# Linear attention's queries and keys as a 1024-column unit by row form, turned on PE

## The chip, the cores and the metric

The kernel runs on one core of a Trainium2 chip. The metric is the device time of one execution in microseconds (us): the median of three runs, 2145.22 us for the kernel before (2144.92 to 2146.12).

The engines are named as the profile names them: PE multiplies matrices (PEld is its weight load), DVE and ACT work elementwise, POOL is used for small work and for issuing DMAs that add, SP issues the loads. PE writes to PSUM, which has eight banks of 128 partitions x 512 words.

## The reference

Two layers over a residual stream x of 256 rows and 2048 columns, all in float32:

```python
def hybrid_layer(x, ...):
    h = rms_norm(x, attn_norm)
    proj = h @ w_in                       # 2048 x 6160
    g_q, g_k, g_v, g_gate, g_lr, s_q, s_k, s_v = split(proj)
    #  512, 512, 1024, 1024,  16, 1024, 1024, 1024 columns
    log_a = log_sigmoid(g_lr @ w_gate_up + b_gate) / 16
    o_gla = gla_chunked(g_q, g_k, g_v, log_a)       # 8 heads, chunks of 64 rows
    o_gla = rms_norm(o_gla, gla_out_norm) * silu(g_gate)
    sq, sk = rms_norm(s_q, sb_q_norm), rms_norm(s_k, sb_k_norm)
    o_sb = rms_norm(stick_breaking_attention(sq, sk, s_v), sb_out_norm)
    x = x + concat(o_gla, o_sb) @ w_o
    hm = rms_norm(x, mlp_norm)
    return x + square(relu(hm @ w_up)) @ w_down     # 2048 -> 8192 -> 2048
```

Linear attention needs its queries and keys with the head's 64 columns on the partitions, multiplied by exponentials of the running sum of log_a: q by exp(b), k by exp(-b), and k by exp(b_last - b).

## The kernel before, in words

**Products.** Every float32 factor is split in a high part (ACT copies it, rounded, into `whi`) and a low part (DVE subtracts, into `wlo`). A product of a 128 x 128 block of h with a 128 x 512 block of weights is three matmuls: high x high, high x low, low x high.

**Plain units** (`unit`, lines 577 to 579) make 256 rows x up to 512 columns of a projection: 16 blocks of h's columns, two halves of rows, three matmuls, so 96 matmuls. A unit loads four blocks of 1 MB and has eight chunks of 12 matmuls. After each chunk `tick()` runs what `after(n, fn)` has put n chunks later: attention's own steps lie between the chunks in this way. The order of PE, DVE and ACT here is that of the tile scheduler.

**The column form** (`unit_t`, lines 624 and 628) makes 256 columns of linear attention's queries or keys already turned: weights are the stationary factor, the high and low parts of h stand side by side as one 512-column moving factor, and the low weights meet the high part in a 256-column matmul. That is 32 pairs of a 512- and a 256-column matmul. `join` adds the two halves (a copy on ACT, an addition on DVE).

**The ordered lists.** The gate, the output projection and the MLP of a layer, and in layer 0 two units for layer 1 ("iv": stick-breaking values, "ik": its keys), run as units of 1024 columns whose order on PE, DVE and ACT is planned (`Plan`: each piece has a length, dependencies and a due time; PE's and SP's pieces keep their order, DVE's and ACT's go by due time) and written out by hand (`manual_schedule`). `STEPS` is the order of the steps of the eight pairs of blocks of such a unit. For a pair in `FAST` (1, 3, 5, 6) seven products stand for eight: DVE makes sums of weight blocks (line 1097), and the operand keeps sums of its own blocks (`forms`, lines 436 to 454). For a pair in `ADDED` (2, 7) the low part is made without DVE: ACT writes the negated high part (line 1274, `dlo`), and a DMA issued by POOL adds the weights to it (line 1277). So a unit has 64 products less 4: 180 matmuls. Three buffers `raw` and two `raw2` hold loaded weights, five `whi` and four `wlo` the parts. Each unit ends in a tail: DVE combines the eight banks, and for "iv" and "ik" ACT multiplies by the row's inverse norm.

**Layer 0's mixer** begins the program: x comes in four parts of 512 columns, each is turned on PE (line 469) and split, between the first chunks. Its units in order: stick-breaking values (512), keys (512), gate rank with the first queries (272), queries (256), values, keys, queries (512 each), four column-form units, linear attention's values (two of 512), and half of the output gate. Layer 1's mixer is the same without values and keys, which "iv" and "ik" have left. The gates' exponentials are multiplied by the row's inverse norm on POOL, for which `row_of` turns that norm into a row on PE (line 535).

Squares for the heads' norms are made in `head_sums` (line 645) on DVE; normalised queries and keys (line 651) are turned on PE (line 688).

Of the kernel before, what the change touches and what calls it, by code (L numbers as in the profile page):

```python
# [17 lines left out]
P = 128  # L18
# [5 lines left out]
FAST = (1, 3, 5, 6)  # L24
ADDED = (2, 7)
BIG = ("up", "down", "iv", "ik")
# [16 lines left out]
C_SQ, C_SK, C_SV = 3088, 4112, 5136  # L43

# [100 lines left out]
def trunk_kernel(  # L145
# [60 lines left out]
    ATT = ("wg", "ident16", "mask16", "tri", "nones", "gmask", "reset", "v4", "lr", "lrT", "ha", "hh", "hl", "hA", "on", "dec", "S", "kdz", "row", "bc")  # L206
# [15 lines left out]
    def mlp_psum():  # L222

        open_scope("psum", m=1)
        unused.update((m, new_bank(m)) for m in (1, 6, 5, 7, 2, 4, 3, 8))
# [5 lines left out]
    open_scope("sbuf", att=1)  # L231
# [99 lines left out]
    def load_small():  # L331
        load_gains(1, (
            ("sq", sb_q_norm, 1), ("sk", sb_k_norm, 1), ("mlp", mlp_norm, KT),
            ("gla", gla_out_norm, 1), ("so", sb_out_norm, 1),
        ))
        load_gate_up(0)
# [85 lines left out]
    def forms(op, i, t, tag):  # L422
# [18 lines left out]
        def high():  # L441
# [6 lines left out]
            todo.append((op.pair(i), t))  # L448
# [9 lines left out]
    def operand_parts(op, n, h2, key, l, place):  # L458
# [30 lines left out]
        def scaled():  # L489
            t = tmp("t2", [P, 2, T], bufs=T2)  # L490
# [6 lines left out]
    def norm_operand(op, n, key, l, sums=False):  # L497
        for h2 in range(2):
            turn, high, low, scaled = operand_parts(op, n, h2, key, l, ps_tile)
            turn()  # L500
            if sums and fast(2 * n + h2):
                for part in forms(op, 2 * n + h2, scaled(), "sxh"):
                    part()
            else:
                high()
                low()
# [288 lines left out]
    hT = Operand()  # L795
    ssq = new_ssq()
    st = {}
    his = []
    load_x(0, parts=2)
    load_gains(0, (("attn", attn_norm, KT),))  # L800
    wait_on_x(WARM0)
    first = [operand_parts(hT, 0, h2, "attn", 0, ps_tile) for h2 in range(2)]
    for turn, _, _, _ in first:
        turn()
    st["first"] = turn_gains(0)
    for _, high, low, _ in first:
        high()
        low()
    wait_on_x(WARM1)

    for l in range(DEPTH):
        wl = w_in[l]
        mixed = Operand()
        nxt = {}

        if l == 0:
            hooks = {}

            def next_x(n):
                load_x(n)  # L820
                with tc.issue_after(st["mm"]):
                    norm_operand(hT, n, "attn", 0)

            for n, at in ((1, (0, 0)), (2, (0, 1)), (3, (1, 1))):
                hooks[at] = lambda n=n: next_x(n)

            def begin():
                st["rst"] = norm_finish(ssq)

            for n in range(4):  # L830
                after(6 + n, lambda n=n: norm_squares(n, ssq))
            after(10, begin)
            after(2, build_constants)
            after(7, load_small)
            after(11, finish_small)
            uv = unit(
                hT, wl, 0, C_SV, 512, hooks=hooks, fine=1,
                order=lambda i, k: his[4 * i + (3 if i else max(1, k))],
            )
            v = tmp("v4", [P, NT, 512], bufs=2)  # L840
            after(3, lambda a=uv, b=v: values(a, b))
        else:
            open_scope("sbuf", att=1)
            att_psum()
            load_gate_up(l)
            after(2, build_constants)
            v = natural["iv"][0]

        def sb_heads(g, qT, kT, v, first):

            state = {}

            def scores(hp):
                state[hp] = sb_scores(qT, kT, 2 * hp)
                after(3, lambda: weights(hp))

            def weights(hp):
                state[hp] = sb_weights(*state[hp])
                after(1, lambda: outs(hp))

            def outs(hp):
                po = ps_tile()
                for j in range(2):
                    sb_out(po, j, state[hp], v, 2 * hp + j)
                o = norm_pair(po)
                after(3, lambda: to_operand(mixed, 4 + 2 * g + hp, o, gain("so", l)))

            for hp in range(2):
                after(first[hp], lambda hp=hp: scores(hp))


        if l == 0:
            uk = unit(hT, wl, 0, C_SK, 512)
            rst = st["rst"]
            kT = act_tile(F32)
            sb_qk(uk, 0, 4, 0, rst, None, kT, 4)
        else:
            rst = st["rst"]
            kT = act_tile(F32)
            after(2, lambda kT=kT: sb_qk(None, 0, 4, 0, rst, None, kT, 5, natural["ik"][0]))  # L880
# [22 lines left out]
        def gates(b):  # L903
# [24 lines left out]
            def fl(t):  # L928
                return t[:, bs, :].rearrange("p e t -> p (e t)")
# [788 lines left out]
```

## Time and profile before

| what | value |
|---|---|
| runs | 2144.92, 2145.22, 2146.12 us |
| profiled execution | 2145.51 us, span 2143.8 us |
| mixer of layer 0 (without its first unit) | 33.9 to 295.9 us of the span |
| list of layer 0, up to the first steps of layer 1's values | 295.9 to 1080.4 us |
| mixer of layer 1 | 1162.6 to 1360.2 us |
| list of layer 1 | 1360.2 to 2139.7 us |
| clock granted to TensorE | 1.00 throughout |
| mean DMA rate | 224 GB/s |

A row of a timeline has the start in us from the span's beginning, the length in us, engine, line, operation, written tile <- read tiles, shapes and count; in brackets the idle time before it and what ended it. A matmul's length overlaps the next one's: what it costs PE is the distance to the next start. A row of stage times has the stretch, its length, and the busy time and count of each engine, then granted clock, share of the DMA engines and GB/s. In a row of waits stand the total, the number and the longest.

### The profile page before, as it was taken

The numbers are of one execution on the slowest core, as the hardware profiler recorded it, in microseconds if no ns is written. First come the engines' busy times: TensorE is split into PE (matmuls) and PEld (weight loads), VectorE is DVE, ScalarE is ACT, GpSimd is POOL, SyncE is SP. The second block draws the span as 40 slices with busy tenths as digits, with TensorE's granted clock in tenths as the row PEclk, the third lists the DMA queues.
The fourth block names the chain that finished last, engine by engine and source line by source line (L and its number), as shares of the span: only waits on it lengthen the run. The fifth ranks groups of instructions, "written<-read, shape, count | busy, mean of one in ns | idle before, by whom it ended". The sixth has DMA issues, their size and how long they took to land.

```text
span 2143.8 us, 28392 instructions
## 1 busy us (share of the span) xinstructions
PE 2134.1 (100%) x10239; PEld 1780.4 (83%) x10239; DVE 1892.3 (88%) x2533; ACT 1471.4 (69%) x1889; POOL 157.0 (7%) x210
## 2 busy tenths in 40 slices
PE   9999999999999999999999999999999999999999
PEld 7988888888888888888878888888888888888887
DVE  5677669999999999999998875799999999999998
ACT  5555456678677677678776654667876776776775
POOL 0020000000000000000001200000000000000000
PEclk9999999999999999999999999999999999999999
DMA  6655456688888888888886544657888888888886
GB/s 229 196 158 167 158 197 196 196 245 265 244 253 246 260 251 243 273 236 255 238 242 170 176 159 158 202 173 228 253 243 274 236 261 247 248 247 253 255 249 182
DMA packets 169105, 480.37 MB, mean 224 GB/s; under 512 B 9370, under 2 KB 34530, under 8 KB 168964
## 3 DMA queue, kind: packets, MB, share of 16 engines
q1 hardware_dynamic: 149380, 407.24, 56.4%
q0 software_dynamic: 19584, 71.31, 17.6%
q8 instruction: 80, 1.31, 0.2%
q14 instruction: 61, 0.50, 0.1%
HBM read 405.12 MB, written 2.10 MB: 190 GB/s over the span
## 4 chain that ended last, share of the span: by engine, by line
PE 94%; DVE 3%; issue 1%; ACT 1%; DMA 0%; POOL 0%; DVEq 0%; ACTq 0%
PE acc L577 4%; PE acc L579 4%; PE acc L578 4%; PE acc L624 3%; PE acc L628 1%; DVE wlo L1268 1%; DVE wlo L560 0%; DVE xb L1097 0%; PE ps L1065 0%; DMA raw<-in_w_in_dram 0%; PE ps L1058 0%; PE ps L742 0%; PE ps L1015 0%; PE ps L688 0%; PE ps L706 0%
## 5 line engine op out<-in xcount | busy, mean ns | idle before, releaser
L1264 ACT ACTIVATE whi<-raw 128x1024 fp32r<-128x1024 f32 (+1 forms) x768 | 738.9, 976 | 314.4 <-issue 45.3
L1268 DVE TENSOR_TENSOR wlo<-raw,whi 128x1024 fp32r<-128x1024 f32 (+1 forms) x632 | 689.1, 1097 | 65.6 <-ACT whi L1264 54.0
L560 DVE TENSOR_TENSOR wlo<-raw,whi 128x1024 fp32r<-128x1024 f32 (+2 forms) x162 | 182.2, 1131 | 93.3 <-ACT whi L558 93.2
L558 ACT ACTIVATE whi<-raw 128x1024 fp32r<-128x1024 f32 (+2 forms) x162 | 156.0, 968 | 153.4 <-PE acc L579 109.3
L1277 POOL DMA_DIRECT2D dlo<-raw x136 | 117.2, 862 | 1587.6 <-ACT dlo L1274 837.7
L1264 ACT ACTIVATE whi<-ts 128x1024 fp32r<-128x1024 f32 x144 | 152.7, 1061 | 73.6 <-DVE ts L1097 4.0
L577 PE MATMUL acc<-whi,act 128*128 128x512 f32 (+2 forms) x512 | 191.4, 374 | 0.0
L578 PE MATMUL acc<-wlo,act 128*128 128x512 f32 (+2 forms) x512 | 186.5, 364 | 0.1
L579 PE MATMUL acc<-whi,act 128*128 128x512 f32 (+2 forms) x512 | 186.5, 364 | 0.0
L1268 DVE TENSOR_TENSOR wlo<-ts,whi 128x1024 fp32r<-128x1024 f32 x144 | 175.5, 1219 | 10.2 <-ACT whi L1264 8.5
L1097 DVE TENSOR_TENSOR ts<-raw 128x1024 f32<-128x1024 f32 x144 | 175.6, 1220 | 1.6
L1274 ACT ACTIVATE dlo<-raw 128x1024 fp32r<-128x1024 f32 x136 | 139.0, 1044 | 3.6 <-PE m__1930_9320 L1378 1.7
L577 PEld LDWEIGHTS acc<-whi,act 128*128 128x128 f32 x512 | 96.7, 189 | 17.5 <-issue 2.7
L579 PEld LDWEIGHTS acc<-whi,act 128*128 128x128 f32 x512 | 96.4, 188 | 15.5
L578 PEld LDWEIGHTS acc<-wlo,act 128*128 128x128 f32 x512 | 96.6, 189 | 14.2 <-DVE wlo L560 0.6
L1097 DVE TENSOR_TENSOR raw<-raw 128x512 f32<-128x512 f32 x144 | 98.9, 687 | 2.3
L1097 DVE TENSOR_TENSOR raw<-ts,raw 128x512 f32<-128x512 f32 x144 | 98.6, 684 | 0.5
L624 PE MATMUL acc<-act,whi 128*128 128x512 f32 x256 | 91.9, 401 | 0.0
L628 PE MATMUL acc<-act,wlo 128*128 128x256 f32 x256 | 71.6, 280 | 0.0
L1469 ACT ACTIVATE act<-act,st 128x512 f32<-128x512 f32 x72 | 49.0, 712 | 19.2 <-DVE act L1097 19.2
L454 DVE TENSOR_TENSOR act<-t,act 128x512 fp32r<-128x512 f32 x84 | 57.0, 683 | 0.0
L624 PEld LDWEIGHTS acc<-act,whi 128*128 128x128 f32 x256 | 48.1, 188 | 10.7
(3145 smaller groups left out, 5333.1 us busy)
## 6 DMA issues: line engine op xcount, KB each, us to landing
raw<-in_w_up_dram SPq DMA_DIRECT2D x112, 1024.0 KB, 5.7
raw<-in_w_down_dram SPq DMA_DIRECT2D x112, 1024.0 KB, 5.9
raw<-in_w_in_dram SPq DMA_DIRECT2D x82, 1024.0 KB, 5.3
dlo<-raw POOLq DMA_DIRECT2D x136, 512.0 KB, 6.5
raw<-in_w_o_dram SPq DMA_DIRECT2D x32, 1024.0 KB, 5.1
raw<-in_w_up_dram SPq DMA_DIRECT2D x32, 512.0 KB, 6.3
raw<-in_w_down_dram SPq DMA_DIRECT2D x32, 512.0 KB, 6.5
raw<-in_w_in_dram SPq DMA_DIRECT2D x18, 512.0 KB, 5.9
```

Of the source, the lines that this page charges most:

```text
L558: newest["hi"] = nc.scalar.activation(h, r, AF.Copy).ins
L560: newest["lo"] = nc.vector.tensor_tensor(lo[:, q : q + step, :width], r, f32(h), ALU.subtract).ins
L577: nc.tensor.matmul(o, xh[:, sl], whi[:, j, :width], start=first, stop=False)
L578: nc.tensor.matmul(o, xh[:, sl], wlo[:, j, :width], start=False, stop=False)
L579: st["mm"] = nc.tensor.matmul(o, xl[:, sl], whi[:, j, :width], start=False, stop=last).ins
L624: nc.tensor.matmul(acc[:, f, :], whi[:, j, sl], op.both(k), start=(k == 0), stop=False, skip_group_check=True,)
L628: nc.tensor.matmul(acc[:, f, T:], wlo[:, j, sl], xh, start=False, stop=(k == KT - 1), skip_group_check=True,)
L1097: nc.vector.tensor_tensor(dst, a, b, op)
L1264: nc.scalar.activation(box["h"][:, :n], src(), AF.Copy)
L1268: nc.vector.tensor_tensor(box["l"][:, :n], src(), f32(box["h"][:, :n]), ALU.subtract)
L1274: nc.scalar.activation(box["l"], src(), AF.Copy, scale=-1.0)
L1277: nc.gpsimd.dma_start(f32(box["l"]), src(), accum_op=ALU.add)
```

## The change

Linear attention's queries and keys, 1024 columns side by side in `w_in`, become a unit of an ordered list ("iq", row form, same fast pairs) and are turned on PE afterwards, by four transposes for each pair of 128 columns (`turned_pair`). DVE multiplies from the bank by the exponentials (`gla_queries`, `gla_keys`), in place: the exponentials have tiles of their own (`eg`). The row's inverse norm is multiplied in the unit's tail, so `row_of` and the multiplications on POOL go.

The list is a function, `ordered(l, units, ...)`. For l = -1 it holds stick-breaking keys and "iq" for layer 0 and stands behind one plain unit, the first 512 columns of linear attention's values (kept in `natural["gv"]`, scaled later). x's fast pairs are kept unsplit (`turned0`: ACT copies them once more from the bank), and their sums are made as the list starts. In layer 0's list "iq" follows "ik". Layer 0's mixer then is: gate rank with first queries, queries (256), values, queries, values (512 each), linear attention's second values, half of the gate; layer 1's is the same without the two values, with both of linear attention's. Layer 1's value unit, which follows a "down" unit, uses a shorter list of steps in which pair 5 is plain (`FEWER`). Also: squares in `head_sums` go to ACT; x's squares are taken earlier; the order in which the list's banks lie over the mixer's depends on the layer; small loads and gate weights of layer 0 are loaded at the start of its mixer; second keys are normalised from two chunks behind the 256-column queries' unit (layer 1: four before).

The diff, cut, without changes of indentation alone:

```diff
+FEWER = [0, 0, 1, 1, 1, 2, 3, 1, 3, 2, 3, 3, 4, 4, 5, 5, 6, 6, 6, 6, 7, 7], (1, 3, 6)
-BIG = ("up", "down", "iv", "ik")
+BIG = ("up", "down", "iv", "ik", "iq")
+AHEAD = {"iv": C_SV, "ik": C_SK, "iq": C_GQ}
...
     def head_sums(ss, src, nh):
-        nc.vector.tensor_tensor(sq[:, : nh * P], src, src, ALU.mult)
+        nc.scalar.activation(sq[:, : nh * P], src, AF.Square)
...
+    def layer_units(l):
+        units = []
+        if l >= 0:
+            units = [("g", 0, 0), ("o", 0, 0), ("o", 0, 1)]
+            units += [(k, q, n2) for q in range(4) for k in ("up", "down") for n2 in range(2)]
+        if l + 1 < DEPTH:
+            units += [("iv", 0, 0)] * (l >= 0) + [("ik", 0, 0), ("iq", 0, 0)]
+        return units
...
-            return STEPS, FAST
+            return FEWER if u and units[u - 1][0] == "down" and kind == "iv" else (STEPS, FAST)
...
+        opened = [gate_done[0, 1]] if l < 0 else []
+        if l < 0:
+            for i in FAST:
+                done["ik", 0, i] = made(
+                    lambda i=i: forms(hT, i, turned0[i], None), None, True, before[-2]
+                )
...
+    u0 = unit(
+        hT, w_in[0], 0, C_GV, 512, hooks=hooks, fine=1,
+        order=lambda i, k: his[4 * i + (3 if i else max(1, k))],
+    )
+    natural["gv"] = act_tile(F32, (P, NT, 512))
+    ordered(-1, layer_units(-1), hT, None, u0, [natural["gv"]])
...
-            uk = unit(hT, wl, 0, C_SK, 512)
-            sb_qk(uk, 0, 4, 0, rst, None, kT, 4)
...
+        after(2, lambda: keys(0, 5))
...
-            gt["row"] = row_of(rst)
...
-            rb = gt["row"].unsqueeze(1).to_broadcast([P, 2, T])
-            for t in (eb, enb, ekd):
-                nc.gpsimd.tensor_tensor(t[:, bs, :], t[:, bs, :], rb, ALU.mult)
...
-        for b in range(2):
-            t = join(unit_t(hT, wl, C_GQ + b * 256))
...
-        for b in range(2):
-            t = join(unit_t(hT, wl, C_GK + b * 256))
...
+        def turned_pair(part, b):
+            nat, pt = natural["iq"][part], ps_tile()
+            for f in range(2):
+                for tt in range(NT):
+                    c = (2 * b + f) * P
+                    nc.tensor.transpose(
+                        pt[:, f * T + tt * P : f * T + (tt + 1) * P],
+                        nat[:, tt, c : c + P], ident,
+                    )
+            return pt.rearrange("p (f t) -> p f t", t=T), slice(2 * b, 2 * b + 2)
...
+        def gla_keys(b):
+            t, bs = turned_pair(1, b)
+            for e in gt["e"][1:]:
+                nc.vector.tensor_tensor(e[:, bs, :], t, e[:, bs, :], ALU.mult)
...
+        for b in range(2):
+            after(1 + 2 * b, lambda b=b: gates(b))
+            after(6 + 2 * b, lambda b=b: gla_keys(b))
+            after(9 + 3 * b, lambda b=b: gla_queries(b))
...
+        after(2, lambda: keys(1, 3))
...
         for tt in range(NT):
-            after(1 + tt, lambda tt=tt: turn_k(tt))
+            after((3 if l else 1) + tt, lambda tt=tt: turn_k(tt))
```

More of the change, by code (lines that the diff above doesn't have):

```diff
@@ L220, in trunk_kernel, with mlp_psum @@
     unused = {}
-    def mlp_psum():
+    def mlp_psum(first):
+        order = (1, 6, 5, 7) if first else (5, 7, 1, 6)
         open_scope("psum", m=1)
-        unused.update((m, new_bank(m)) for m in (1, 6, 5, 7, 2, 4, 3, 8))
+        unused.update((m, new_bank(m)) for m in (*order, 2, 4, 3, 8))
     def bank(m):
@@ L487, in low, with scaled @@
                 )
[L489 to L490 removed]
+        def scaled(t=None):
+            t = tmp("t2", [P, 2, T], bufs=T2) if t is None else t
             for j, (src, g) in enumerate(got):
@@ new lines, in layer_units, with ordered @@
+    def layer_units(l):
[6 more added lines that the diff above has]
+        return units
+    natural = {}
+    def ordered(l, units, hT, rst, ug, gates_t, mixed=None, ons=None):
+        ahead = l + 1 < DEPTH
+        wl = w_in[max(l, 0)]
+        wn = w_in[l + 1] if ahead else None
@@ L1454, in sums @@
                 box["s"] = (c, b, a, d)
-            into = kind not in ("iv", "ik")
+            into = kind not in AHEAD
             if not into:
```

547 lines of the change are left out of this document (271 added, 276 removed).

## The prediction

> **What bounds the kernel now.** I read the page first (busy shares and the chain that ended last), then what PE waited for, then the busy times by stage, and last the order of time where the change cuts in.
>
> ```profile
> span 2143.8 us, 28392 instructions
> ...
> PE 2134.1 (100%) x10239; PEld 1780.4 (83%) x10239; DVE 1892.3 (88%) x2533; ACT 1471.4 (69%) x1889; POOL 157.0 (7%) x210
> ...
> PE 94%; DVE 3%; issue 1%; ACT 1%; DMA 0%; POOL 0%; DVEq 0%; ACTq 0%
> ```
>
> PE is the bound from end to end: 94% of the chain that ended last is PE. A busy PE proves little by itself, so the next view is what it waited for.
>
> ```profile
> PE ps L688 <- DVE act L651: 2.1, 3, 1.6
> ...
> PE m__2025_9760 L1378 <- DVE wlo L1268: 0.6, 1, 0.6
> PE m__2028_9771 L1378 <- DVE wlo L1268: 0.5, 1, 0.5
> ```
>
> The rows left out are of the first 4 us. So PE waits little, and for DVE. So a change is worth what it takes from PE's stream of instructions, less the new places at which DVE, or something behind it, is late. The busy times by stage say how near DVE is (start and end; length; busy time of PE, PEld, DVE, ACT, POOL). The rows are layer 0's mixer behind its first unit, layer 0's ordered list, and layer 1's mixer.
>
> ```profile
> 33.90:295.90 262.00, 261.66 (x1472) 222.26 (x1471) 174.81 (x269) 130.24 (x189) 16.18 (x22) 1.00 0.53 169
> 295.90:1080.40 784.50, 784.40 (x3561) 651.36 (x3560) 742.01 (x954) 584.17 (x725) 56.96 (x66) 1.00 0.81 242
> 1162.60:1360.20 197.60, 195.58 (x1181) 167.81 (x1180) 147.03 (x242) 101.36 (x156) 15.08 (x21) 1.00 0.52 167
> ...
> 1202.00:1226.00 24.00, 22.03 (x120) 18.23 (x119) 23.51 (x37) 16.71 (x29) 6.40 (x5) 1.00 0.33 103
> ```
>
> DVE is 95% busy in the list (742 of 784.5) and PE does not wait there; in layer 1's mixer it is 74% busy on average but 98% in 1202 to 1226, and there lies the 1.6 us wait.
>
> **The change, part by part.** First the prices on PE, as the distance between starts.
>
> ```profile
> 699.73 0.39 PE L1379 MATMUL m__1220_6014<-whi,act 128*128 128x512 f32 x1
> ...
> 702.90 0.39 PE L1378 MATMUL m__1297_6366<-wlo,act 128*128 128x512 f32 x1
> ...
> 1079.63 0.60 PE L469 MATMUL m__2007_9685<-ident,xb 128*128 128x128 f32 x4
> 1080.06 0.60 PE L469 MATMUL m__2009_9694<-ident,xb 128*128 128x128 f32 x4
> 1080.42 0.48 PE L1377 MATMUL m__2011_9701<-whi,act 128*128 128x512 f32 x1
> 1080.73 0.39 PE L1378 MATMUL m__2011_9701<-wlo,act 128*128 128x512 f32 x1
> ...
> 1245.83 0.39 PE L624 MATMUL acc<-act,whi 128*128 128x512 f32 x1
> ...
> 1249.99 0.39 PE L624 MATMUL acc<-act,whi 128*128 128x512 f32 x1
> ```
>
> Fourteen 512-column matmuls of the list take 702.90 - 699.73 = 3.17 us, 0.2264 each. Twelve pairs of the column form (a 512 and a 256) take 4.16 us, 0.3467 a pair. Four transposes take 0.43, and the first matmul behind transposes costs 0.31 - 0.23 = 0.08 more.
>
> 1. Queries and keys. The column form has 32 pairs a unit, four units a layer, two layers: 256 x 0.3467 = 88.8 us go. The new unit has 64 products of three matmuls, less four by its four fast pairs: 180 a layer, 360 x 0.2264 = 81.5 come. It must be turned: 8 groups of four transposes, 8 x (0.43 + 0.08) = 4.1 come. Net -3.2.
> 2. Layer 0's keys leave two plain units (192 matmuls, 43.5) for a unit of 180 (40.8): -2.7.
> 3. The short list makes pair 5 of layer 1's value unit plain: 3 matmuls more, +0.7.
> 4. The row of scales (L535) goes with its multiplications on POOL: four transposes and their waits, some -0.6.
>
> PE's stream so shortens by 5.8 us. By a rule of the Trainium skill (TensorE: Matmul & The Clock Gate, Back-to-back issue gap) an isolated matmul is N / 2.4 + 2.5 ns apart, 215.8 and 109.2 ns here. By that the three units cost 117.2 instead of 122.9 and the removed ones 83.2 and 41.4, and the stream shortens by 3.9. The rows say 226 ns, and are used.
>
> 5. What the short list is worth on the other side: with four fast pairs, DVE was late in this unit.
>
> ```profile
> 1108.80 0.39 PE L1377 MATMUL m__2028_9771<-whi,act 128*128 128x512 f32 x1
> 1109.65 0.50 PE L1378 MATMUL m__2028_9771<-wlo,act 128*128 128x512 f32 x1 [0.46 <-DVE wlo L1268]
> ...
> 1111.60 0.40 PE L1377 MATMUL m__2025_9760<-whi,act 128*128 128x512 f32 x1
> 1112.59 0.50 PE L1378 MATMUL m__2025_9760<-wlo,act 128*128 128x512 f32 x1 [0.59 <-DVE wlo L1268]
> ```
>
> (0.85 - 0.23) + (0.99 - 0.23) = 1.4 us of wait. A plain pair needs two subtractions of 1.2 on DVE where a fast one needs three and a half and three additions, so over 4 us of DVE are saved and the wait goes: -1.4 (from 0 to -1.4).
>
> 6. The new list in front of layer 0, behind one plain unit, starts with nothing made in advance. The prices are from the start of layer 0's list, from its last part on DVE, and from the additions by DMA.
>
> ```profile
> 296.14 0.69 ACT L1142 ACTIVATE act<-acc,st 128x512 f32<-128x512 f32 x1 [1.94 <-PE acc L579]
> 296.72 1.05 ACT L1264 ACTIVATE whi<-raw 128x1024 fp32r<-128x1024 f32 x1
> 297.67 0.68 ACT L1142 ACTIVATE act<-acc,st 128x512 f32<-128x512 f32 x1
> ...
> 314.89 0.62 ACT L450 ACTIVATE act<-t 128x512 fp32r<-128x512 f32 x1
> ...
> 1091.23 0.69 DVE L1097 TENSOR_TENSOR raw<-raw 128x512 f32<-128x512 f32 x1
> 1091.83 1.22 DVE L1268 TENSOR_TENSOR wlo<-ts,whi 128x1024 fp32r<-128x1024 f32 x1
> 1092.97 0.28 DVE L436 TENSOR_TENSOR t<-t 128x128 f32<-128x128 f32 x1
> ...
> 1094.02 1.22 DVE L1268 TENSOR_TENSOR wlo<-raw,whi 128x1024 fp32r<-128x1024 f32 x1
> ```
> ```profile
> L1274 ACT ACTIVATE dlo<-raw x136: 1039/1043/1063, 401.7 to 2123.4; 128x1024 fp32r<-128x1024 f32 x136
> L1277 POOL DMA_DIRECT2D dlo<-raw x136: 850/859/1016, 403.1 to 2124.7; - x136
> ...
> DMA to landing us min/median/max: 4.5/6.5/11.7
> ```
>
> ACT takes its queue in order, and in the new program one copy into whi stands ahead of the copy out of the first unit's bank and the rest behind it. After the first unit's last matmul ACT has, by starts: copy 0.58, whi 0.95, copy 0.58, a form 0.6, two whi 1.9, then the first negated copy 1.04: 5.7 us. POOL issues 0.3 later (403.1 - 401.7 - 1.04), and the addition lands 6.5 after that, at 12.5. PE has 42 matmuls (9.5) and one more (0.2) before it needs it: a wait of 2.8. Beside this runs DVE: up to the last pair it has 18 passes of 1.13, 15 of 0.6 and three groups of small sums of 1.05, 32.5 us, and cannot begin before 1.7; PE wants the last of it 33.3 us after that first unit (153 matmuls less the last six), so DVE alone holds PE back by about 1. The larger one counts: +2.8. Bounds: 1 (addition in time, DVE alone) to 8 (landing 11.7). Behind it DVE gains on PE: a unit of this kind takes it some 35 us against 40.8. Its weights are loaded during the first unit, on SP's queue behind that unit's own. The eight scaled copies that keep the operand's fast pairs, and the squares of x, now earlier, lie in the first unit on ACT:
>
> ```profile
> 20.00:31.00 11.00, 11.00 (x54) 9.20 (x53) 7.33 (x10) 8.16 (x17) 0.00 (x0) 1.00 0.80 271
> ```
>
> ACT has 2.8 us in 11 to spare there, and a copy of half a bank costs it some 0.4: hidden, and 0.4 for each that finds no room.
>
> 7. The seam from this list to the mixer, new in layer 0, has its like at 1162.6, for which the waits have no row. I take +0.3, the smaller of the two idle times below, for one late subtraction; bounds 0 and the 2.3 of that place.
>
> 8. Moves. The squares for the norms of heads go from DVE to ACT:
>
> ```profile
> 33.90:295.90 262.00, 11.36 (x18) 1.00 0.53 169
> 1162.60:1360.20 197.60, 11.83 (x18) 1.00 0.52 167
> ```
>
> 11.8 us less for DVE in layer 1, and with 16 subtractions of 1.2 and four joins of 0.7 (as the additions above) fewer it has some 113 us of work left (147 - 12 - 19.5 - 2.8) in 155 (197.6 less half of 88.8, plus 2): 73%, as before. ACT gets 93 in 155, 60% instead of 51%. So the mixers are shorter, not denser on DVE; the squares cost nothing while ACT has that room, else about 0.6 each.
>
> Layer 1's second keys begin two chunks earlier. Their transposes wait now:
>
> ```profile
> 1215.80 0.39 PE L579 MATMUL acc<-whi,act 128*128 128x512 f32 x1
> 1217.83 0.33 PE L688 MATMUL ps<-ident,act 128*128 128x128 f32 x1 [1.64 <-DVE act L651]
> 1218.43 0.55 PE L688 MATMUL ps<-ident,act 128*128 128x128 f32 x3 [0.27 <-DVE act L651]
> ```
>
> Between starts that is (2.03 - 0.23) + (0.60 - 0.11) = 2.3 us. The chain from squares to transposes stays as long in chunks, but DVE has two passes less in it; I take half as gone, -1.2, bounds 0 and -2.3. The small loads (gains) go behind the third load of the mixer's first unit on SP, the gate weights behind the fourth; they are used a unit later. SP loads 24 blocks of 1 MB less and 24 more. POOL loses twelve multiplications and gets twelve issues of 0.86 (it is 7% busy). None of this is on the path while the seam holds; gains that came late would stop the first queries, within the 2.3 above.
>
> Sum: -5.8 - 1.4 + 2.8 + 0.3 - 1.2 = -5.3. The profiled execution took 2145.5 (span 2143.8), the median of the runs is 2145.2; so 2140.2 for such an execution and **2139.9** for the median.
>
> **The rivals.**
> - Heads crowd the shorter mixers: slower. Keys and queries come late to their transposes as at L688, at four of the ten units that are turned (five a layer) besides the one now. Each costs the 2.3 us of that place. For it: DVE at 98% in 1202 to 1226, and attention's steps now share chunks with linear attention's. Against: 73% on average. With the old wait kept, the sum is -4.1, so two more (4.6) decide; with four, 2145.2 - 4.1 + 9.2 = 2150.
> - The new list stays behind: additions land at 11.7, PE waits 8 instead of 2.8, and the gain is gone: 2145.2 - 5.3 + 5.2 = 2145. For it: first units of the list have no stock. Against: fewer transfers beside it than in steady state.
> - All covers hold: the additions land as fast as the fastest row, DVE alone counts (1), the seam costs nothing, and the wait at L688 goes whole: 2145.2 - 5.8 - 1.4 + 1 - 2.3 = 2136.7. A rule of the Trainium skill (DMA: Bandwidth & Descriptors, Anatomy of one DMA — SWDGE (gpsimd) path) goes this way: 2.0 us + bytes / 436e3, 3.2 us for 512 KB. The trace disagrees: its fastest is 4.5.
>
> **How the numbers follow.** Forecast 0.47, crowded heads 0.18, the list behind 0.17, all covers 0.18. The forecast's own range is 2136 to 2143. The whole range goes from 2134 to 2148: the bounds of the third rival and half of the first. A measurement of this kernel tells about 0.2%, 4.3 us, from no change. Faster than that (under 2140.9): the third rival and three quarters of the forecast, 0.18 + 0.35 = 0.53; within: the rest of the forecast and the second rival, 0.12 + 0.17 = 0.29; slower: the first rival, 0.18.
>
> **What would show it.** Three units more of list matmuls at 0.226, no L624 or L628; a first wait of PE some 10 us behind the first unit, on a dlo, of 2 to 4 us; no wait of PE in the value unit of layer 1; in the mixers DVE under 80%, no PE wait over 2 us on normalised keys. A wait of several us in the mixers, or a second one in the new list, would make it wrong.

## The result, and the profile after

The changed kernel takes 2135.39 us (median of six runs, 2134.72 to 2135.84); the kernel before, run beside it, 2145.67 (2144.92 to 2147.5). The ratio is 0.995 with a 95% interval of 0.994 to 0.996: 10.3 us less, where the prediction had 5.3. The profiled execution took 2135.84 with a span of 2134.1, so its span is 9.7 us shorter. Of the 42 executions of the kernel before that ran beside the experiments below, 17 show a mean granted clock of 0.999 and take 1.4 to 1.9 us more, by medians within a group, than those with 1.000, which all six of the changed kernel show; so a part of the 10.3 us may be clock, while in the two profiled executions the clock is 1.00.

From the page after, the span, the busy times and the chain that ended last:

```profile
span 2134.1 us, 28323 instructions
...
PE 2126.2 (100%) x10106; PEld 1771.3 (83%) x10106; DVE 1913.8 (90%) x2574; ACT 1525.3 (71%) x1976; POOL 150.7 (7%) x206
...
PE 96%; DVE 2%; ACT 1%; issue 0%; DMA 0%; DVEq 0%; ACTq 0%
```

PE's share of the chain rose from 94% to 96% and DVE's fell from 3% to 2%. What PE waits for after (left out are the rows of the first 10 us and one of 0.2 us near the end):

```profile
PE ps L702 <- DVE act L665: 0.8, 1, 0.8
...
PE m__79_428 L1119 <- DMA dlo<-raw: 0.3, 1, 0.3
...
PE m__77_426 L1119 <- DVE wlo L1009: 0.2, 1, 0.2
```

The first row is the keys' wait of before (L688 <- L651 there, 2.1 us), the two others are the new list's. DVE's two waits in layer 1's value unit are gone. The stages after, in the columns of the rows shown of before: the new list, layer 0's mixer behind it, layer 0's list up to layer 1's values, layer 1's mixer.

```profile
34.40:118.10 83.70, 83.16 (x362) 67.11 (x361) 76.49 (x102) 63.15 (x77) 13.01 (x20) 1.00 0.78 216
118.10:291.90 173.80, 173.80 (x1037) 148.59 (x1036) 121.36 (x214) 102.30 (x164) 6.83 (x14) 1.00 0.50 164
291.90:1080.00 788.10, 788.06 (x3582) 654.37 (x3580) 745.85 (x958) 587.88 (x734) 56.03 (x66) 1.00 0.81 242
1197.70:1350.20 152.50, 151.67 (x939) 130.60 (x938) 111.03 (x204) 90.27 (x152) 6.21 (x14) 1.00 0.49 159
```

DVE is busy for 70% and 73% of the two mixers, ACT for 59%, near the 73% and 60% of the prediction's step 8.

PE's busy time does not tell stream from waiting, so I count each stage in another way: the distance from its first matmul's start to the next stage's, less its matmuls at the distances between undisturbed starts (0.227 for 512 columns, 0.118 for 256, 0.124 for 272, 0.109 for a transpose). What is left over is time beyond the stream.

| stage | length before | after | beyond the stream before | after |
|---|---|---|---|---|
| start and first unit | 32.4 | 33.0 | 4.8 | 5.3 |
| list in front of layer 0 | - | 83.7 | - | 1.9 |
| layer 0's mixer | 261.9 | 173.8 | 3.4 | 1.6 |
| layer 0's list, with the units for layer 1 | 866.7 | 905.8 | 2.3 | -0.1 |
| layer 1's mixer | 197.6 | 152.5 | 4.7 | 2.2 |
| layer 1's list | 779.5 | 779.5 | 0.5 | 0.5 |
| sum | 2138.1 | 2128.3 | 15.7 | 11.4 |

The stream went from 2122.4 to 2116.9 us, -5.5, where the prediction had -5.8. (The count takes nearly the prediction's prices, so it tells more of the number of matmuls than of their price.) The time beyond it fell by 4.3, where the prediction had a rise of 0.5 (-1.4 + 2.8 + 0.3 - 1.2). All of the error lies there, and 3.4 of it in the two mixers: they gave 4.3 us, forecast 0.9 (1.2 - 0.3). The experiments ask why.

### The profile page after: what moved, and what is told of

Same layout as the page of the kernel before. It is cut to its first block, busy times and chain, and to the rows that moved or that the text cites. A ratio compares the mean times of both kernels' runs of the same rounds, so it can differ in the third digit from the quotient of the medians.

```text
span 2134.1 us, 28323 instructions
## 1 busy us (share of the span) xinstructions
PE 2126.2 (100%) x10106; PEld 1771.3 (83%) x10106; DVE 1913.8 (90%) x2574; ACT 1525.3 (71%) x1976; POOL 150.7 (7%) x206
## 4 chain that ended last, share of the span: by engine, by line
PE 96%; DVE 2%; ACT 1%; issue 0%; DMA 0%; DVEq 0%; ACTq 0%
PE acc L591 4%; PE acc L593 4%; PE acc L592 4%; DVE wlo L1009 1%; PE ps L1694 0%; PE ps L1687 0%; PE ps L702 0%; PE ps L756 0%; PE ps L1644 0%; PE ps L720 0%; DVE wlo L574 0%; DVE raw L837 0%; DVE ts L837 0%; PE ps L471 0%; PE ps L768 0%
## 5 line engine op out<-in xcount | busy, mean ns | idle before, releaser
L1005 ACT ACTIVATE whi<-raw 128x1024 fp32r<-128x1024 f32 (+1 forms) x827 | 795.8, 976 | 336.6 <-issue 47.2
L1009 DVE TENSOR_TENSOR wlo<-raw,whi 128x1024 fp32r<-128x1024 f32 (+1 forms) x679 | 741.3, 1099 | 89.6 <-ACT whi L1005 77.7
L591 PE MATMUL acc<-whi,act 128*128 128x512 f32 (+2 forms) x448 | 167.0, 373 | 0.0
L574 DVE TENSOR_TENSOR wlo<-raw,whi 128x1024 fp32r<-128x1024 f32 (+2 forms) x114 | 120.0, 1058 | 49.7 <-ACT whi L572 49.2
L572 ACT ACTIVATE whi<-raw 128x1024 fp32r<-128x1024 f32 (+2 forms) x114 | 105.7, 930 | 82.1 <-PE acc L593 75.9
L593 PE MATMUL acc<-whi,act 128*128 128x512 f32 (+2 forms) x448 | 161.8, 361 | 0.0
L592 PE MATMUL acc<-wlo,act 128*128 128x512 f32 (+2 forms) x448 | 161.6, 361 | 0.1
L591 PEld LDWEIGHTS acc<-whi,act 128*128 128x128 f32 x448 | 84.5, 189 | 14.7 <-issue 3.1
L593 PEld LDWEIGHTS acc<-whi,act 128*128 128x128 f32 x448 | 84.5, 189 | 13.1
L452 ACT ACTIVATE act<-t 128x512 fp32r<-128x512 f32 x88 | 54.3, 622 | 0.4 <-DVE t L440 0.3
L660 DVE TENSOR_REDUCE st<-t 128x4 f32<-128x512 f32 (+1 forms) x36 | 21.8, 621 | 7.3 <-ACT t L659 7.0
L837 DVE TENSOR_TENSOR xb<-t,xb 128x512 f32<-128x512 f32 x40 | 27.4, 685 | 0.1
```

The costliest lines, as they stand in the source:

```text
L572: newest["hi"] = nc.scalar.activation(h, r, AF.Copy).ins
L574: newest["lo"] = nc.vector.tensor_tensor(lo[:, q : q + step, :width], r, f32(h), ALU.subtract).ins
L591: nc.tensor.matmul(o, xh[:, sl], whi[:, j, :width], start=first, stop=False)
L592: nc.tensor.matmul(o, xh[:, sl], wlo[:, j, :width], start=False, stop=False)
L593: st["mm"] = nc.tensor.matmul(o, xl[:, sl], whi[:, j, :width], start=False, stop=last).ins
L837: nc.vector.tensor_tensor(dst, a, b, op)
```

## The experiments

Twelve kernels were run in three groups, each beside the kernel before on the same chip, whose median was 2146.09, 2145.99 and 2146.72. "To before" is a median's distance to that one, and runs of different groups are compared by it; the changed kernel has -10.3. The third median lies 0.6 to 0.7 above the others, so the last four rows come out a little too good: straight from the changed kernel's 2135.39 they are 4.3, 0.1, 4.5 and 5.05 us above it. The spans are of one execution each, and the program's start alone (up to the list in front of layer 0) differs between them by 0.7 us (32.4 to 33.1).

| run | median, us | ratio (95%) | to before | span |
|---|---|---|---|---|
| full list for layer 1's values | 2136.80 | 0.9957 (0.9944 to 0.9969) | -9.3 | 2134.9 |
| squares on DVE | 2137.93 | 0.9962 (0.9950 to 0.9975) | -8.2 | 2136.2 |
| late keys | 2134.38 | 0.9947 (0.9934 to 0.9959) | -11.7 | 2133.1 |
| plain pairs first | 2145.83 | 0.9998 (0.9989 to 1.0007) | -0.3 | 2143.8 |
| column units | 2146.32 | 1.0001 (0.9993 to 1.0010) | +0.3 | 2144.4 |
| plain keys in layer 0 | 2138.25 | 0.9965 (0.9953 to 0.9978) | -7.7 | 2138.1 |
| late copies | 2133.89 | 0.9943 (0.9930 to 0.9955) | -12.1 | 2131.7 |
| late copies, late keys | 2133.49 | 0.9940 (0.9927 to 0.9954) | -12.5 | 2130.9 |
| GpSimd reads | 2139.70 | 0.9967 (0.9955 to 0.9980) | -7.0 | 2136.2 |
| GpSimd writes | 2135.51 | 0.9949 (0.9937 to 0.9962) | -11.2 | 2133.8 |
| column units, DVE multiplies | 2139.86 | 0.9969 (0.9957 to 0.9981) | -6.9 | 2138.2 |
| column units, late keys | 2140.44 | 0.9972 (0.9962 to 0.9983) | -6.3 | 2138.7 |

**Full list for layer 1's values.** The short list is undone.

```diff
-            return FEWER if u and units[u - 1][0] == "down" and kind == "iv" else (STEPS, FAST)
+            return STEPS, FAST
```

> The changed kernel, with layer 1's value unit on the long list again (four fast pairs). Theory as forecast (the short list takes away 1.4 us of waiting for DVE and costs three matmuls, 0.7): 0.7 us slower than the changed kernel, 9.6 faster than the kernel before, and two waits of 0.6 to 0.8 us between starts in this unit. Rival (the waits had gone anyway, since PE's other waits shifted): 0.7 faster than the changed kernel, 11.0 faster than before, no wait.

0.8 us more by span, 1.0 by medians. The waits of before are back in PE's rows:

```profile
PE m__2089_9870 L1119 <- DVE wlo L1009: 0.6, 1, 0.6
...
PE m__2092_9881 L1119 <- DVE wlo L1009: 0.3, 1, 0.3
```

Layer 0's list has 1.9 us beyond its stream again, against -0.1, for 0.7 less stream. Steps 3 and 5 of the prediction (+0.7 - 1.4) hold.

**Squares on DVE.** The squares for the heads' norms go back from ACT.

```diff
-        nc.scalar.activation(sq[:, : nh * P], src, AF.Square)
+        nc.vector.tensor_tensor(sq[:, : nh * P], src, src, ALU.mult)
```

> The changed kernel, with the squares of the heads' norms on DVE again (36 of up to 0.69 us). Theory A (DVE's relief is why the mixers lost 3.8 us of waiting: 8.2 - 6.9 in layer 0, 4.7 - 2.2 in layer 1): 2 to 4 us slower than the changed kernel, 6 to 8 faster than before, a wait of about 2 us before the transposes of layer 1's second keys. Theory B (the other place of the keys and the removed row of scales did it): within 1 us of the changed kernel.

2.1 us more, by span and by medians. Layer 0's mixer has 2.4 us beyond its stream instead of 1.6, layer 1's 3.3 instead of 2.2, and the keys wait 1.4 instead of 0.8. So the squares' move was worth some 2 us, about half of what the mixers gave.

**Late keys.** Layer 1's second keys begin four chunks behind their unit, as in the kernel before, instead of two.

```diff
-        after(2, lambda: keys(1, 3))
+        after(4 if l else 2, lambda: keys(1, 3))
```

> The changed kernel, with layer 1's second keys normalised from four chunks behind the 256-column queries' unit, as in the kernel before, instead of two. Theory B (their place decides the wait at their transposes): 1 to 2 us slower than the changed kernel, a wait of about 2 us before these transposes. Theory A (DVE's relief decides): within 0.5 us.

1.0 us less by span, 1.4 by medians (1.0 straight): the keys' wait is gone, and layer 1's mixer has 1.3 us beyond its stream instead of 2.2. The earlier place cost time.

**Plain pairs first.** The new list begins with a plain pair (4) in second place, so that the additions by DMA would have more time.

```diff
+OPENS = [0, 0, 4, 4, 1, 1, 1, 3, 1, 2, 3, 3, 2, 3, 5, 5, 6, 5, 5, 6, 6, 6, 7, 7]
...
+            if l < 0 and u == 0:
+                return OPENS, FAST
```

> The changed kernel, with the two plain pairs first in the list in front of layer 0 (order 0 0 4 4 1 1 1 3 1 2 ...), so that DVE and the first additions by DMA have 5.4 us more before PE needs them. Theory (the 1.9 us of waiting in this list come from its start without a stock): 1.0 to 1.9 us faster than the changed kernel, about 11.8 faster than before. Rival (DVE is the bound of this list all along): within 0.4 us of the changed kernel, the same waits later.

The run refutes both: 10 us more, the whole gain, and all of it in this list (93.4 us instead of 83.7). Given the other order, the planner put the copies and sums for later pairs on ACT and DVE ahead of pair 4's parts. PE's order of time there:

```profile
39.70 0.40 PE L1123 MATMUL m__82_431<-whi,act 128*128 128x512 f32 x1
42.18 0.50 PE L1121 MATMUL m__79_428<-whi,act 128*128 128x512 f32 x1 [2.09 <-ACT whi L1008]
43.97 0.79 PE L1122 MATMUL m__79_428<-wlo,act 128*128 128x512 f32 x1 [1.29 <-DVE wlo L1012]
44.56 0.63 PE L1123 MATMUL m__79_428<-whi,act 128*128 128x512 f32 x1
44.99 0.63 PE L1121 MATMUL m__79_428<-whi,act 128*128 128x512 f32 x1
```

Two waits, with one matmul between them, take 3.8 us (43.97 - 39.70 - 2 x 0.23), and then matmuls start 0.43 apart instead of 0.23. The stage times say why (the column before the last two is the granted clock):

```profile
44.40:47.00 2.60, 2.60 (x7) 2.00 (x7) 2.56 (x5) 2.53 (x5) 0.00 (x0) 0.52 1.06 206
...
79.00:84.00 5.00, 5.00 (x12) 3.94 (x13) 2.96 (x4) 1.19 (x2) 0.00 (x0) 0.50 0.72 206
```

The granted clock fell to half here, and again from 79 us, behind a wait of 3.3 us for an addition by DMA.

**Column units.** Linear attention's queries and keys by column form again, with the row of scales and its multiplications on GpSimd; linear attention's keys are turned where the kernel before turns them (`turn_k`), and everything else is as changed.

```diff
-            units += [("iv", 0, 0)] * (l >= 0) + [("ik", 0, 0), ("iq", 0, 0)]
+            units += [("iv", 0, 0)] * (l >= 0) + [("ik", 0, 0)]
...
+            for t in (eb, enb, ekd):
+                nc.gpsimd.tensor_tensor(t[:, bs, :], t[:, bs, :], rb, ALU.mult)
...
+            t = join(unit_t(hT, wl, C_GQ + b * 256))
...
+            t = join(unit_t(hT, wl, C_GK + b * 256))
```

> One part undone: the linear attention's queries and keys are computed by column form in both mixers again, with the row of scales and its multiplications on GpSimd; layer 0's keys still come from the new list, and the short list and the moved squares stay. Theory (the change's gain is the stream's, row by row): the column form is dearer by the terms of the prediction, 88.8 - 85.6 = 3.2 us in two layers, and the row of scales costs 0.6, so the time is about 3.8 us above the changed kernel's, some 6.5 us under the kernel before (ratio 0.997). Rival (the queries and keys in the list also crowd DVE there, and the mixers without their turnings lose waits): the unit by column form brings some of the list's waits away, and the time is within 1.5 us of the changed kernel's (ratio 0.9955). Third (the column units' splits crowd the mixers' DVE): more than 6 us above the changed kernel's (ratio 0.998 or more).

10.3 us more by span: 3.6 of stream, as the theory has it, and 7.0 beyond it, 6.3 of these in layer 1's mixer. So neither the theory nor the second case, and of the third the size but not the reason. PE's order of time, DVE's and GpSimd's (POOL's), one fence each:

```profile
1212.10 0.30 PE L702 MATMUL ps<-ident,act 128*128 128x128 f32 x1 [4.67 <-DVE act L665]
```
```profile
1205.21 3.45 DVE L574 TENSOR_TENSOR wlo<-raw,whi 128x1024 fp32r<-128x1024 f32 x2
1208.58 1.22 DVE L390 TENSOR_TENSOR st<-st 128x8 f32<-128x8 f32 x1
1209.84 1.19 DVE L391 SCALAR_TENSOR_TENSOR st<-st,st 128x8 f32<-128x8 f32 x1
1211.06 0.17 DVE L392 SCALAR_TENSOR_TENSOR st<-st,st 128x8 f32<-128x8 f32 x1
```
```profile
1205.35 5.65 POOL L1565 TENSOR_TENSOR eg<-eg,row 128x512 f32<-128x512 f32 x3
```

Beside three products of GpSimd, two subtractions take 3.45 us and two steps on eight words a partition 1.2 each. In the changed kernel, without the products, the same steps take:

```profile
1242.41 2.35 DVE L574 TENSOR_TENSOR wlo<-raw,whi 128x1024 fp32r<-128x1024 f32 x2
1244.68 0.15 DVE L390 TENSOR_TENSOR st<-st 128x8 f32<-128x8 f32 x1
1244.87 0.17 DVE L391 SCALAR_TENSOR_TENSOR st<-st,st 128x8 f32<-128x8 f32 x1
```

That is 1.1 + 1.05 + 1.0, some 3.2 us that DVE lost on the way to the keys. The kernel before shows the same beside its second block of products, ahead of its own wait of 1.6 us:

```profile
1209.06 5.22 POOL L945 TENSOR_TENSOR act<-act,row 128x512 f32<-128x512 f32 x3
```
```profile
1207.66 0.67 DVE L645 TENSOR_TENSOR t<-act 128x512 f32<-128x512 f32 x1
...
1209.44 1.47 DVE L645 TENSOR_TENSOR t<-act 128x512 f32<-128x512 f32 x1
1210.83 2.29 DVE L560 TENSOR_TENSOR wlo<-raw,whi 128x1024 fp32r<-128x1024 f32 x1
...
1213.64 1.71 DVE L560 TENSOR_TENSOR wlo<-raw,whi 128x1024 fp32r<-128x1024 f32 x1
...
1215.35 1.21 DVE L560 TENSOR_TENSOR wlo<-raw,whi 128x1024 fp32r<-128x1024 f32 x1
```

0.8 + 1.1 + 0.5 = 2.4 us lost, as much as the 2.3 between starts that PE stood there. The last four runs test this.

**Plain keys in layer 0.** Layer 0's keys are two plain units of its mixer again, and the new list makes only linear attention's queries and keys.

```diff
-            units += [("iv", 0, 0)] * (l >= 0) + [("ik", 0, 0), ("iq", 0, 0)]
+            units += [("iv", 0, 0)] * (l >= 0) + [("ik", 0, 0)] * (l >= 0) + [("iq", 0, 0)]
...
+            plain_keys(0)
```

> One part undone: layer 0's softmax keys are two plain units of its mixer again, and the list in front of layer 0 makes only the linear attention's queries and keys; all else is as in the changed kernel. Theory (rows): 192 matmuls with a third product come back, 43.5 against 40.8 us, so the time is about 2.7 us above the changed kernel's, some 7.6 us under the kernel before (ratio 0.9965); the list's start without stock stays where it is. Rival (the mixer of layer 0 was short of DVE, and the keys' splits in it bring waits): 4 to 6 us above the changed kernel's (ratio 0.9975). Other rival (a list of one unit has no time to gain on its late start, or the mixer hides the third product): within 1 us of the changed kernel's.

2.6 us more by medians: step 2's 2.7. (By span it is 4.0: in the profiled execution, of 2139.81 us, the keys of layer 1 wait 1.6 instead of 0.8.) The list of one unit still has 1.6 us beyond its stream: the start costs what it costs, however long the list.

**Late copies.** In the new list's plan, ACT's copies of the first unit's banks become ready one piece of PE's later.

```diff
-                "ACT", A1, lambda tt=tt: copy_first(tt), before[-2], gate_done.get((0, 0))
+                "ACT", A1, lambda tt=tt: copy_first(tt), before[-1 if l < 0 else -2], gate_done.get((0, 0))
```

> One order changed: in the list in front of layer 0, ACT's first copy of the finished gates stands behind two more splits of weights instead of ahead of them (the copy waits for the end of the first unit, and in the changed kernel's trace ACT stood idle behind it from 31.4 to 34.6 us). Theory (the list's 1.9 us of waits are a start without stock: ACT is held up by the copy, and the splits come late by as much): 1 to 1.9 us under the changed kernel (2133.5 to 2134.4, ratio 0.995 or a little less). Rival (DVE is the bound of the list, 76.5 of 83.7 us busy, and the first halves' additions land when they land): the waits stay where they are or move, and the time is within 0.7 us of the changed kernel's or above it.

1.8 us less by medians, 2.4 by span, of which 0.6 are a shorter start of the program that runs without this edit show too. ACT's order of time in the changed kernel, then in this one:

```profile
30.31 1.15 ACT L1005 ACTIVATE whi<-raw 128x1024 fp32r<-128x1024 f32 x1
34.62 0.60 ACT L877 ACTIVATE act<-acc 128x512 f32<-128x512 f32 x1 [3.16 <-PE acc L593]
35.12 1.05 ACT L1005 ACTIVATE whi<-raw 128x1024 fp32r<-128x1024 f32 x1
```
```profile
29.80 2.10 ACT L1005 ACTIVATE whi<-raw 128x1024 fp32r<-128x1024 f32 x2
...
33.00 1.06 ACT L1005 ACTIVATE whi<-raw 128x1024 fp32r<-128x1024 f32 x1 [0.58 <-DMA raw<-in_w_in_dram]
34.09 0.60 ACT L877 ACTIVATE act<-acc 128x512 f32<-128x512 f32 x1
```

ACT makes three splits of weights ahead of the copy instead of one, and the list takes 81.9 us, 0.1 beyond its stream. So its waits were ACT's late start, and DVE is not its bound.

**Late copies and late keys.** Both edits.

> The late copies and layer 1's second keys two chunks later together. If the two are in different stages and each is worth what its own run showed, the gains add: 1.0 us of the late keys and what the run with late copies alone gives, 2132.5 to 2134.5 (ratio 0.9943). If the list's start is bound by DVE: 2134.4, as with the late keys alone.

2133.49 us, 12.5 under the kernel before: the fastest version run. By medians, of the 1.0 to 1.4 us of the late keys only 0.4 came on top of the late copies (by span 0.8 of 1.0): the late copies alone had already brought the keys' wait from 0.8 to 0.5.

**GpSimd reads.** The changed kernel with three products on GpSimd behind each copy of the decays; nothing reads the result.

```diff
+            dz = tmp("dz", [P, 2, T], bufs=1)
+            for t in (eb, enb, ekd):
+                nc.gpsimd.tensor_tensor(dz, t[:, bs, :], t[:, bs, :], ALU.mult)
```

> The changed kernel, with GpSimd multiplying again where the kernel before did: three products of 128x512 behind each of the two copies of the decays in a mixer, twelve in all, into a scratch tile that nothing reads. Nothing else is changed, PE, DVE and ACT have the same instructions in the same order. Theory (the two engines share a way to SBUF, and DVE's passes with two operands in SBUF are stretched while GpSimd reads: in the run with column units two subtractions took 3.45 us instead of 2.35 and two steps of 0.16 us took 1.2 each beside these products): DVE loses 1 to 1.9 us at each block, the wait for layer 1's second keys grows from 0.8 us to 2 to 5, and the time is 2 to 4.5 us above the changed kernel's (2137.5 to 2140, ratio about 0.997). Rival (GpSimd's products are hidden, as the prediction had it, and the column units' long wait came from the units): within 0.7 us of the changed kernel's.

2.1 us more by span, 3.3 by medians (4.3 straight). Two executions, the profiled one (2138.22) and one of 2138.58, have a granted clock of 1.000; the other three have 0.999 and take 2139.70 to 2140.53. Layer 1's mixer alone is longer, 154.8 us instead of 152.5. PE's wait, DVE and GpSimd there:

```profile
PE ps L702 <- DVE act L665: 3.1, 1, 3.1
```
```profile
1241.89 3.19 DVE L574 TENSOR_TENSOR wlo<-raw,whi 128x1024 fp32r<-128x1024 f32 x2
1245.01 1.00 DVE L390 TENSOR_TENSOR st<-st 128x8 f32<-128x8 f32 x1
1246.05 0.17 DVE L391 SCALAR_TENSOR_TENSOR st<-st,st 128x8 f32<-128x8 f32 x1
1246.25 0.89 DVE L392 SCALAR_TENSOR_TENSOR st<-st,st 128x8 f32<-128x8 f32 x1
```
```profile
1241.92 5.20 POOL L1564 TENSOR_TENSOR dz<-eg 128x512 f32<-128x512 f32 x3
```

DVE loses 0.8 + 0.85 + 0.7 = 2.4 us, and PE's wait grows by 2.3. The work of PE, DVE and ACT is unchanged, so GpSimd's products do this by themselves. In layer 0's mixer the same products cost nothing: 1.6 us beyond the stream, as without them.

**GpSimd writes.** The control, with fills in the place of products.

```diff
+            for _ in range(8):
+                nc.gpsimd.memset(dz, 0.0)
```

> The control to the run before: at the same places GpSimd writes only, eight fills of 128x512 each time instead of three products, into the same kind of scratch tile. Theory (it is GpSimd's reading that stretches DVE): DVE's passes keep their 1.2 and 0.16 us beside the fills, and the time is within 0.7 us of the changed kernel's. Rival (any work of GpSimd on SBUF stretches DVE): like the products, 2 us or more above the changed kernel's.

0.3 us under the changed kernel by span, 0.1 above it by medians straight: no cost. The fills depend on nothing, so they ran at the start of the mixers and not at the products' place; there they stand beside DVE's subtractions of two operands too. GpSimd and DVE in layer 0:

```profile
117.93 9.33 POOL L1564 MEMSET dz<- 128x512 f32 x16 [7.11 <-PE m__167_838 L1119]
```
```profile
119.84 0.71 DVE L574 TENSOR_TENSOR wlo<-raw,whi 128x544 fp32r<-128x544 f32 x1
```

In the changed kernel that subtraction takes 0.72. So writing does not stretch these passes; that fills at the products' own place would not either wasn't tried. Other passes of DVE are stretched there: beside the fills three 128x128 casts take 0.36, 0.29 and 0.62 us instead of 0.22 each, and a TENSOR_SCALAR on eight words a partition 0.38 instead of 0.17, all at a place where PE does not wait for them.

**Column units, DVE multiplies.** As the column units, with the twelve products on DVE.

```diff
-                nc.gpsimd.tensor_tensor(t[:, bs, :], t[:, bs, :], rb, ALU.mult)
+                nc.vector.tensor_tensor(t[:, bs, :], t[:, bs, :], rb, ALU.mult)
```

> The run with column units, but the twelve products with the row of scales are DVE's own, 0.69 us each by DVE's rows, instead of GpSimd's. Theory (in that run GpSimd's blocks cost DVE more than its own products would: 3.2 us lost beside the second block, against 3 x 0.69 = 2.1): the wait for layer 1's second keys is about 1 us shorter than the 4.7 there, and the time is 1 to 3 us under the 2146.3 of that run (2143 to 2145). Rival (DVE is short of time there, and GpSimd's help is worth its price): the wait grows by 1 us or more, and the time is 2147 or more.

6.2 us less than the column units by span, 7.2 by medians, far more than the theory had: the wait of 4.7 us falls to 0.3, and with it the slow clock behind it. Here twelve passes more on DVE are cheaper than GpSimd's twelve products. Against the changed kernel it has 3.4 us more by medians (4.5 straight), and 4.1 by span: the 3.6 of stream and 0.5.

**Column units, late keys.** As the column units, with layer 1's keys four chunks behind their unit.

```diff
-        after(2, lambda: keys(1, 3))
+        after(4 if l else 2, lambda: keys(1, 3))
```

> The run with column units, and layer 1's second keys two chunks later, where the kernel before has them. Theory (of the 10.9 us that the column units cost, 3.8 are stream, and the rest is layer 1's wait of 4.7 us with the slow clock behind it, which comes of keys too early for a stretched DVE): the wait falls under 2.5 us, the clock stays whole behind it, and the time is 2139 to 2142. Rival (the column units' own work crowds the mixers wherever the keys are): the waits move and the time stays above 2143.5.

The theory's case: 5.7 us less than the column units by span, 6.6 by medians, a wait of 0.3, no slow clock. The second block of GpSimd's products still stretches passes on the way to the keys:

```profile
1205.51 3.77 POOL L1565 TENSOR_TENSOR eg<-eg,row 128x512 f32<-128x512 f32 x3
```
```profile
1206.01 0.83 DVE L383 TENSOR_SCALAR st<-st 128x8 f32<-128x8 f32 x1
1208.06 2.31 DVE L574 TENSOR_TENSOR wlo<-raw,whi 128x1024 fp32r<-128x1024 f32 x1 [1.22 <-ACT whi L572]
```

0.17 and 1.22 are the lengths without products. But the transposes now stand later in PE's order, and PE comes to them at 1212.5, when the keys are all but ready (the last pass begins at 1211.89). So the later place hides the loss; it does not avoid it.

## Why the prediction was right or wrong

- **The stream (steps 1, 2, 4): right.** -5.5 against -5.8. Undone one by one, layer 0's keys cost 2.6 us (forecast 2.7), and queries, keys and row of scales 3.4 to 4.5 with GpSimd out of the way, 3.6 of it stream by count (forecast 3.2 + 0.6).
- **The short list (3 and 5): right.** 1.0 us by medians, forecast 0.7; all of layer 0's list went from 2.3 us beyond its stream to -0.1, where step 5 had 1.4.
- **The new list's start (6): right in mechanism in part, and too dear.** +1.9 us against +2.8. Only 0.5 of it is the wait for an addition that the step priced; the rest are short waits for low parts from DVE (`wlo`), up to 0.3 each. POOL's issues of the first additions and PE's first matmul with one, after:

```profile
40.33 1.92 POOL L1018 DMA_DIRECT2D dlo<-raw  x2 [38.95 <-ACT dlo L1015]
```
```profile
44.63 0.40 PE L1118 MATMUL m__79_428<-whi,act 128*128 128x512 f32 x1
45.34 0.51 PE L1119 MATMUL m__79_428<-dlo,act 128*128 128x512 f32 x1 [0.31 <-DMA dlo<-raw]
```

  The issue is 5.9 us behind the unit's end, as the step's sum has it (5.7 + 0.3), but the matmul starts 5.0 later, not 6.5 (the median of the kernel before; this first one landed near the fastest, 4.5). The step's floor of 1 us from DVE was wrong: with ACT's start mended nothing is left.
- **The seam (7): a stall that was not there.** Layer 0's mixer came out at 1.6 us beyond its stream, from 3.4, and from 115 to 300 us PE's view of waits has no row.
- **The moves (8): right by luck at the wait that it priced, too small around it.** It had -1.2 for that wait, and the two mixers gave 4.3. At the keys after the change:

```profile
1244.89 0.39 PE L592 MATMUL acc<-wlo,act 128*128 128x512 f32 x1
1246.11 0.30 PE L702 MATMUL ps<-ident,act 128*128 128x128 f32 x1 [0.83 <-DVE act L665]
```

  PE stands 1.22 - 0.23 = 1.0 us between starts, from 2.3: -1.3, as forecast. But three effects meet here and the step knew one. With the squares back on DVE the wait grows by 0.6. "POOL loses twelve multiplications ... None of this is on the path" was wrong: with products back it grows by 2.3, and the time by 2.1 by span and 3.3 by medians, though GpSimd is 7% busy. The keys' earlier place, taken to leave the chain as it was, costs 1.0 to 1.4. A cost that the step did not see made up for a part of a gain that it did not see. Each was undone alone, so the three need not add. In the kernel before, the passes ahead of L688 lost 2.4 us beside GpSimd's products, but those products alone do not make its wait of 2.1: with products, keys at the old place and squares on ACT (the last run) it is 0.3. How much of the 2.1 is due to each of the two isn't split by these runs.

  The other 3.0 us of the mixers lie outside this wait, where the step had nothing. The squares, which "cost nothing" on ACT, were credited only through half a wait; with them back on DVE layer 0's mixer loses 0.8 and layer 1's 1.1, half of that outside the wait. And the three runs with column units all have 1.0 to 1.1 us more beyond the stream in layer 0's mixer than the changed kernel, whoever multiplies by the row of scales. So there the column units cost more than step 1's sum. Their price is one reason: step 1 took 0.3467 a pair from twelve in a row, while the 237 pairs of the kernel before that follow each other directly are 0.356 apart on the mean (most 0.34 to 0.36, sixteen 0.43). How much comes of that, and how much of what goes with these units, is open.
- **The rivals.** The measured 2135.39 lies 0.6 us under the forecast's own range (2136 to 2143), and the gain is nearly twice the forecast. The result lies nearest to "all covers hold" (2136.7), and its reasons hold in part: the first addition came near the fastest row, the seam cost nothing, the wait at L688 fell from 2.1 to 0.8. It did not know of GpSimd either. "Heads crowd the shorter mixers" does not occur here, but it is real: with GpSimd's products beside them the keys waited 4.7 us. "The new list stays behind" is what another order of steps does, by ACT's and DVE's order and not by a slow landing alone.
- **What would show it.** No wait in layer 1's values, DVE under 80% in the mixers, no wait over 2 us on normalised keys: all so. The first wait on a `dlo` came 10 us behind the first unit as said, but took 0.5 us between starts and not 2 to 4. (One row that the prediction left out of its view of waits, of 0.2 us, is not of the first 4 us but lies at some 2100 us; nothing hangs on it.)

## What to carry to other kernels

An engine that is 7% busy can lengthen a wait that the profile puts down to another: where a waiting pass belongs to an engine with room to spare, compare the length of its passes there with their length elsewhere, and see which engine works beside the long ones. When work is taken off a path, price what its absence does to its neighbours too. At the start of a list, look for an engine whose queue has a waiting copy in front of work that could run.

## What the runs showed of the hardware

GpSimd's products of 128x512 in SBUF stretch DVE's passes with two operands in SBUF: 2.35 us for two subtractions became 3.19 and 3.45, and steps of 0.16 took 0.9 to 1.2. Fills by GpSimd left a subtraction of half the size at 0.71, where it takes 0.72 without them (but they did stretch casts of 0.22 to as much as 0.62). The Trainium skill says this (SBUF — State Buffer, Who interferes with whom): a DVE instruction with two inputs in SBUF contends with a GpSimd instruction that reads SBUF, not with one that only writes it. The subtractions agree with both halves.

The granted clock fell to 0.5 behind three stalls of PE: 3.8 us (two waits with one matmul between), 3.3 us, and 4.7 us in the column units' run, where the 2.7 us behind the wait show:

```profile
1212.10:1214.80 2.70, 2.70 (x10) 2.28 (x11) 2.28 (x3) 0.00 (x0) 0.00 (x0) 0.54 0.02 3
```

In the profiled execution a wait of 3.1 us (GpSimd reads) left it at 1.00:

```profile
1247.90:1252.00 4.10, 3.99 (x34) 3.89 (x35) 3.71 (x6) 1.38 (x3) 1.41 (x4) 1.00 0.00 0
```

The Trainium skill (TensorE: Matmul & The Clock Gate, Part 1: The HAM clock gate) has the gate look at windows of some 3.4 us that run freely, and halve the clock after an idle one; these four stalls are near that length. Three of the five executions of the kernel with GpSimd's reads show 0.999 over the whole, which would fit a stall that halves the clock in some executions and not in others; no trace of those three is kept.
